# 64-slot experts: fp32 weights fed unsplit into two halves of the array's columns, and expert weights laid out in rows of 8 KB

## The chip, the cores and the metric

The kernel runs on one core of a Trainium2 chip. The metric is the device time of one execution in microseconds (us), as a median of runs; lower is better. The engines are PE (TensorE matmuls; PEld is its loading of the stationary operand), DVE (VectorE), ACT (ScalarE), POOL (GpSimd) and SP (SyncE, which here issues the DMAs).

## The reference: what is computed

Two layers on 256 frames of width 1024: a mixer (attention, short convolution and a gated recurrence) and then a channel mixer. The channel mixer of layer 0 is a dense SwiGLU, that of layer 1 has eight experts of which each frame takes two:

```python
def swiglu(x, w_gate, w_up, w_down):
    return (jax.nn.silu(x @ w_gate) * (x @ w_up)) @ w_down
...
    logits = (t @ w_router).astype(jnp.float32) + b_router.astype(jnp.float32)
    top_v, top_i = lax.top_k(logits, TOP_K)
    top_w = jax.nn.softmax(top_v, axis=-1)
    gates = jnp.sum(jax.nn.one_hot(top_i, N_EXPERTS, dtype=jnp.float32) * top_w[..., None], axis=1)
    for e in range(N_EXPERTS):
        out = out + gates[:, e:e + 1].astype(t.dtype) * swiglu(t, w_gate[e], w_up[e], w_down[e])
```

Per expert w_gate and w_up are 1024 x 3584 and w_down is 3584 x 1024, all fp32: 42 MB (of 1,048,576 bytes each) per expert, 336 MB for eight. That is most of what the kernel reads.

## The kernel before

**Stages.** From 0 to about 160 us runs mixer 0, to about 400 us the dense channel mixer, to about 540 us mixer 1, and from there to the end the experts (`moe`). All weights pass through one `Stream` (line 46): a list of halves of 1 MB (128 partitions x 2048 fp32) in the order in which they are used. `load` (L71) issues the next half on SP's queue as soon as a raw buffer is free. `high` (L99, its work at L107) rounds a half to fp32r on ACT (tile `whi`), `low` (L109, its work at L117) takes the remainder on DVE (tile `wlo`) and then frees the raw buffer. `get` (L123) is called ahead of each piece of matmuls and keeps `low` 2.5 and `high` 3.5 halves ahead of what PE uses; there are 4 `whi` and 3 `wlo` tiles. In the expert stage the raw buffers are 3 of `raw`, 4 blocks `b0` to `b3` and, for a time, `x3`, `x4` and `y`.

**Experts by rank.** `route` counts the frames of each expert and sorts them. The three fullest (`r < NBIG`) have 128 slots, the other five 64. An expert is done in 7 blocks of 512 hidden columns: 21 big and 35 small blocks. `plan_moe` (L808) puts three big blocks first and then spreads the other big ones between the small ones; the steps of neighbouring blocks interleave as gate of block i, up of block i-1, down of block i-2. The PE, ACT and DVE order of this stage is the order of the code (`manual_schedule`).

**A big block** takes the product of two split operands as three fp32r products (hi x hi, lo x hi, hi x lo). Gate and up are 24 matmuls each of 512 moving columns, down 24, so 72.

**A small block** packs the hi and lo parts of its 64 slots side by side into the 128 columns of the stationary operand (`gather`, `gather2`), so two products do: each k-tile of a weight goes through as `whi` and as `wlo`, 128x512 each. Gate 16, up 16, down 16 matmuls: 48. The two halves of 64 rows in the result have to be added: `gate` and `up_done` copy both results to SBUF (`a`, `au`), `turn` (L1002) multiplies them with a matrix of two stacked identities (`both`), which transposes and adds, and then computes silu times up on 64 columns and splits that into hi and lo again (L1018 to L1022). `down_piece` uses two banks (`ls`), and `finish` (L1036) scales them (L1043, L1044), scatters them back with 16 matmuls and adds to `xT` (L1053).

**Layout.** w_gate and w_up lie as in the reference; a half is 128 partitions x 4 k-tiles x 512 columns, so runs of 2 KB in HBM. A half of w_down is 128 partitions x 2 rows x 1024 columns, runs of 4 KB.

Of the kernel before, what the change touches and what calls it, by code (L numbers as in the profile page):

```python
# [16 lines left out]
P = 128  # L17
# [28 lines left out]
class Stream:  # L46

    def __init__(self, nc, raw, parts):  # L50
        self.nc, self.parts = nc, parts


        self.free = [(lambda: raw.tile([P, 2048], F32, name="raw"), None)] * RAW_BUFS
# [5 lines left out]
    def add(self, *halves, fine=False, wide=False):  # L60


        self.src += [(x, fine, wide) for x in halves]
        return len(self.src) // 2 - 1
# [6 lines left out]
    def load(self):  # L71
        while self.free and self.n_load < len(self.src):
            x, fine, _ = self.src[self.n_load]
# [35 lines left out]
    def low(self):  # L109
# [8 lines left out]
        if h:  # L118
            buf = self.raw.pop(i)[1]
            if buf[1] is None or self.n_load + len(self.free) < buf[1]:  # L120
                self.free.append(buf)

    def get(self, c, h):  # L123
# [6 lines left out]
        while self.n_hi < min(n + 2 * (HI_BUFS - LO_BUFS), last):  # L130
            self.high()
        n = self.hi[i].shape[1] // 2
        return self.hi[i][:, q * n:(q + 1) * n], self.lo[i][:, q * n:(q + 1) * n]


class Kern:
    def __init__(self, tc, ctx, d):
# [3 lines left out]
        self.raw = ctx.enter_context(tc.tile_pool(name="rawp", bufs=RAW_BUFS))  # L141
# [10 lines left out]
    MOE_TAGS = dict(z=2, lv=2, ls=2, S=2)  # L152
# [659 lines left out]
    def plan_moe(self, j):  # L812
# [3 lines left out]

        d = self.d
# [13 lines left out]
        def half(w, r, i, n, c):  # L831

            def view(e):
                x = w[j].rearrange("e (k p) c -> e p k c", p=P)[e, :, i:i + n, c]
                return x if r == 0 else x.rearrange("e p k c -> (e p) k c")
# [4 lines left out]
        for kind, i in steps:  # L840
            r, b = blocks[i]
            if kind != "d":
                w = d["moe_w_gate" if kind == "g" else "moe_w_up"]
                halves = (half(w, r, q, 4, slice(b * 512, (b + 1) * 512)) for q in (0, 4))
            else:
                halves = (half(d["moe_w_down"], r, 4 * b + q, 2, slice(0, D)) for q in (0, 2))
            plan[kind, r, b] = self.st.add(*halves, fine=(kind, i) == ("d", n - 1),
                                           wide=(kind, i) not in (("g", 0), ("d", n - 1)))
        return blocks, steps, plan

    def moe(self, l, plan, z):
        nc, tc = self.nc, self.tc
        blocks, steps, plan = plan
        with ExitStack() as ctx:
# [8 lines left out]
            self.st.more(lambda: spare(xbuf(4)), 2 * plan["d", 1, 3] + 2)  # L863

# [14 lines left out]
            both = big.tile([P, 64], F32, name="both")  # L879
            nc.vector.tensor_tensor(both, self.ident[:, 0:64], self.ident[:, 64:P], ALU.add)  # L880
# [17 lines left out]
            def rows(k, n, rhs):  # L898

                pg = self.bank()  # L900
                for j in range(2):
                    for t in range(2):
                        self.mm(pg[:, j * T:(j + 1) * T], (hth, htl)[n][:, t, (k + j) * P:(k + j + 1) * P], rhs(t),
                                t == 0, t == 1)
# [15 lines left out]
            def gather(ranks):  # L920

                for r, x in ranks:
                    xs[r] = xbuf(x) if r < NBIG else xbuf(x)[:, 0]

                def step(k, n):
                    pv = rows(k, n, lambda t: S[:, t].rearrange("p a b -> p (a b)"))
                    pv = pv.rearrange("p (j a b) -> p j a b", j=2, a=2)
                    for i, (r, _) in enumerate(ranks):
                        if r >= NBIG:
                            nc.scalar.activation(xs[r][:, k:k + 2, n * 64:(n + 1) * 64], pv[:, :, i, 0:64], AF.Copy)  # L930
# [9 lines left out]
            def gather2():  # L940

                pair = [xbuf(1), xbuf(2)]
                for r in range(NBIG, NE - 1):
                    xs[r] = pair[(r - NBIG) // 2][:, (r - NBIG) % 2]

                def step(k, n):
                    pv = rows(k, n, lambda t: S2[:, t, :, 0:64])
                    pv = pv.rearrange("p (j a b) -> p a j b", j=2, a=4)
                    for m in range(2):
                        nc.scalar.activation(pair[m][:, :, k:k + 2, n * 64:(n + 1) * 64], pv[:, 2 * m:2 * m + 2],  # L950
                                             AF.Copy)
# [485 lines left out]
```

## Time and profile before

| | us |
|---|---|
| median of 3 runs (lowest to highest) | 1440.64 (1440.03 to 1442.37) |
| the profiled execution's own time | 1441.26 |
| its span in the trace | 1439.5 |
| PE busy in the span | 1393.2 (97%) |
| DVE busy | 1221.7 (85%) |
| ACT busy | 1029.7 (72%) |
| bytes read | 433.20 MB, 302 GB/s over the span |

The busy shares of the page are over the whole span. The three stages ahead of the experts use the DMA queue little and the expert stage uses it without a pause, so the stages have to be read one by one. A PE that is shown busy overlaps the end of one matmul with the start of the next; how far apart matmuls start is read from the chain of work or from the timeline.

### The profile page before, as it was taken

The numbers are of one execution on the slowest core, as the hardware profiler recorded it, in microseconds if no ns is written. First come the engines' busy times: TensorE is split into PE (matmuls) and PEld (weight loads), VectorE is DVE, ScalarE is ACT, GpSimd is POOL, SyncE is SP. The second block draws the span as 40 slices with busy tenths as digits, with TensorE's granted clock in tenths as the row PEclk, the third lists the DMA queues.
The fourth block names the chain that finished last, engine by engine and source line by source line (L and its number), as shares of the span: only waits on it lengthen the run. The fifth ranks groups of instructions, "written<-read, shape, count | busy, mean of one in ns | idle before, by whom it ended". The sixth has DMA issues, their size and how long they took to land.

```text
span 1439.5 us, 21728 instructions
## 1 busy us (share of the span) xinstructions
PE 1393.2 (97%) x8323; PEld 1200.9 (83%) x8323; DVE 1221.7 (85%) x1216; ACT 1029.7 (72%) x1062; POOL 19.6 (1%) x39
## 2 busy tenths in 40 slices
PE   7999999999999997999999999999999999999997
PEld 7887999999999886787787887878888788877875
DVE  8967765555587678899989999998999999999997
ACT  8556643344474646788888788888888888888884
POOL 4000000000000000000000000000000000000000
PEclk9999999999999999999999999999999999999999
DMA  7333455555552375899999999999999999999993
GB/s 271 128 104 127 148 195 177 186 194 176 178 173 92 122 257 205 320 396 410 409 394 388 379 394 411 413 411 392 402 412 410 400 411 411 413 411 411 412 412 152
DMA packets 186766, 435.73 MB, mean 303 GB/s; under 512 B 6816, under 2 KB 11040, under 8 KB 186656
## 3 DMA queue, kind: packets, MB, share of 16 engines
q1 hardware_dynamic: 186656, 434.28, 80.0%
q8 instruction: 67, 1.10, 0.3%
q14 instruction: 43, 0.35, 0.1%
HBM read 433.20 MB, written 1.05 MB: 302 GB/s over the span
## 4 chain that ended last, share of the span: by engine, by line
PE 81%; DVE 10%; DMA 3%; ACT 2%; issue 2%; DVEq 0%; ACTq 0%
PE z L356 49%; PE S L356 12%; PE lv L356 11%; PE ls L356 7%; DVE wlo L117 5%; DMA b<-moe_w_gate 3%; ACT whi L107 1%; PE S L1007 1%; DVE y L1044 1%; DVE xT L1053 0%; DVE b L549 0%; DVE on L533 0%; PE lv L659 0%; PE S L659 0%; DVE al L1019 0%
## 5 line engine op out<-in xcount | busy, mean ns | idle before, releaser
L117 DVE TENSOR_TENSOR wlo<-raw,whi 128x1024 fp32r<-128x1024 f32 (+2 forms) x287 | 479.7, 1684 | 96.1 <-issue 50.2
L107 ACT ACTIVATE whi<-raw 128x1024 fp32r<-128x1024 f32 (+2 forms) x287 | 404.4, 1427 | 176.0 <-PE z L356 101.7
L117 DVE TENSOR_TENSOR wlo<-b,whi 128x2048 fp32r<-128x2048 f32 (+1 forms) x177 | 395.6, 2249 | 10.8 <-PE z L356 4.2
L356 PE MATMUL z<-whi,x 128*128 128x512 f32 x1232 | 366.0, 400 | 3.5 <-DVE x L936 2.6
L107 ACT ACTIVATE whi<-b 128x2048 fp32r<-128x2048 f32 (+1 forms) x177 | 332.9, 1883 | 33.9 <-PE z L356 8.9
L356 PE MATMUL z<-wlo,x 128*128 128x512 f32 x896 | 282.7, 396 | 4.6 <-DVE wlo L117 4.3
L356 PEld LDWEIGHTS z<-whi,x 128*128 128x128 f32 x1232 | 224.4, 189 | 50.3 <-DVE x L936 3.1
L356 PE MATMUL z<-hi,whi 128*128 128x256 f32 x864 | 246.5, 286 | 9.6 <-ACT whi L107 7.9
L356 PE MATMUL z<-lo,whi 128*128 128x256 f32 x864 | 246.7, 286 | 0.0
L356 PE MATMUL z<-hi,wlo 128*128 128x256 f32 x864 | 245.9, 285 | 0.0
L356 PEld LDWEIGHTS z<-wlo,x 128*128 128x128 f32 x896 | 167.3, 188 | 49.9 <-DVE wlo L117 9.9
L356 PEld LDWEIGHTS z<-hi,whi 128*128 128x128 f32 x864 | 164.1, 190 | 12.3 <-ACT whi L107 7.9
L356 PEld LDWEIGHTS z<-hi,wlo 128*128 128x128 f32 x864 | 164.0, 190 | 2.9 <-issue 2.1
L356 PEld LDWEIGHTS z<-lo,whi 128*128 128x128 f32 x864 | 164.1, 190 | 2.5 <-issue 1.3
L356 PE MATMUL ls<-whi,ah 128*128 128x512 f32 x264 | 83.8, 396 | 0.0
L356 PE MATMUL ls<-wlo,ah 128*128 128x512 f32 x264 | 83.6, 395 | 0.0
L356 PEld LDWEIGHTS ls<-wlo,ah 128*128 128x128 f32 x264 | 49.6, 188 | 12.0
L356 PEld LDWEIGHTS ls<-whi,ah 128*128 128x128 f32 x264 | 49.3, 188 | 11.6
L117 DVE TENSOR_TENSOR wlo<-x,whi 128x2048 fp32r<-128x2048 f32 x24 | 54.6, 2286 | 3.4 <-PE z L356 3.0
L356 PE MATMUL lv<-whi,ah 128*128 128x512 f32 x168 | 53.3, 395 | 0.0
L356 PE MATMUL lv<-wlo,ah 128*128 128x512 f32 x168 | 53.3, 395 | 0.0
L356 PE MATMUL lv<-whi,al 128*128 128x512 f32 x168 | 53.3, 395 | 0.0
(332 smaller groups left out, 1712.1 us busy)
## 6 DMA issues: line engine op xcount, KB each, us to landing
b<-moe_w_gate SPq DMA_DIRECT2D x59, 1024.0 KB, 9.6
b<-moe_w_up SPq DMA_DIRECT2D x57, 1024.0 KB, 10.3
b<-moe_w_down SPq DMA_DIRECT2D x56, 1024.0 KB, 10.0
raw<-moe_w_up SPq DMA_DIRECT2D x45, 1024.0 KB, 10.3
raw<-moe_w_down SPq DMA_DIRECT2D x43, 1024.0 KB, 9.6
raw<-moe_w_gate SPq DMA_DIRECT2D x42, 1024.0 KB, 9.5
raw<-w_in SPq DMA_DIRECT2D x22, 1024.0 KB, 4.9
raw<-ffn_w_gate SPq DMA_DIRECT2D x14, 1024.0 KB, 5.0
```

Of the source, the lines that this page charges most:

```text
L107: self.nc.scalar.activation(hi, x, AF.Copy)
L117: self.nc.vector.tensor_tensor(lo, x, self.hi[i][:, h * a:(h + 1) * a].bitcast(F32), ALU.subtract)
L356: self.nc.tensor.matmul(out, lhsT, rhs, start=start, stop=stop, skip_group_check=True)
L1007: nc.tensor.transpose(pt[:, q * P:(q + 1) * P], a[0][:, q * P:(q + 1) * P], self.ident)
L1044: nc.vector.scalar_tensor_tensor(y2[:, 1, c], y[c], gs[:, 0:1], y2[:, 0, c].bitcast(F32), ALU.mult, ALU.subtract)
```

## The change

It touches the expert stage and the host's layout of its weights.

1. **Layout.** The host stores each half of an expert's weight as 128 partitions x 2048 fp32 in one piece, so a partition's part is one run of 8 KB. The values are the same. In the program the DMA of a half is now 128x2048 where it was 128x4x512 or 128x2x1024. The last block's down weights still load in four parts of 0.5 MB.
2. **Small blocks take the raw fp32 weight.** `whole=True` halves are neither rounded nor split: `part` returns nothing for them, `get` returns the raw buffer, and a new `done` frees it behind PE's last matmul on it. The slots are gathered as plain fp32, 64 columns wide. For gate and up each k-tile is two matmuls with the same 64 stationary columns, one for weight columns 0 to 255 into rows 0 to 63 of the bank and one for columns 256 to 511 into rows 64 to 127: the two halves of the array's columns. For down, the two halves are the two 512-column halves of the output, in one bank.
3. **What falls away in a small block**: both splits of each weight half, the copies `a`/`au` of 512 columns, the matmuls with `both`, the hi/lo split of the activations. What comes: Silu on ACT and the product with up on DVE at once on 128x256, two transposes, one copy.
4. **Buffers.** `x2` is one more raw buffer for the whole expert stage. `ls` has one bank, `S` three.

```diff
     def part(self, n, parts, name):
         i, h = divmod(n, 2)
+        if self.src[i][3]:
+            return None, None
...
-        if h:
-            buf = self.raw.pop(i)[1]
-            if buf[1] is None or self.n_load + len(self.free) < buf[1]:
-                self.free.append(buf)
+        if h and not self.src[i][3]:
+            self.release(i)
+
+    def release(self, i):
+        buf = self.raw.pop(i)[1]
+        if buf[1] is None or self.n_load + len(self.free) < buf[1]:
+            self.free.append(buf)
...
+        if self.src[i][3]:
+            n = self.raw[i][0].shape[1] // 2
+            return self.raw[i][0][:, q * n:(q + 1) * n]
...
+    def done(self, c, h):
+        if h % 2:
+            self.release(2 * c + h // 2)
+            self.load()
...
-    MOE_TAGS = dict(z=2, lv=2, ls=2, S=2)
+    MOE_TAGS = dict(z=2, lv=2, ls=1, S=3)
...
+            self.st.more(lambda: spare(xbuf(2)))
...
+                w = self.st.get(c, h)
+                for k in ks:
+                    for i in range(2):
+                        self.mm(z[i * 64:(i + 1) * 64, 0:256], xs[r][:, k], w[:, k - 2 * h, i * 256:(i + 1) * 256],
+                                k == 0, k == KT - 1)
+                self.st.done(c, h)
...
             def gate(r, z):
+                n = 512 if r < NBIG else 256
+                a = tp.tile([P, 512], F32, name="a", bufs=2)[:, 0:n]
+                nc.scalar.activation(a, z[:, 0:n], AF.Silu, scale=sTs[r][1][:, 1:2])
+                return a
...
+                for q in range(4 if r < NBIG else 2):
+                    nc.tensor.transpose(pt[:, q * P:(q + 1) * P], a[:, q * P:(q + 1) * P], self.ident)
...
-                pv = pt.rearrange("p (m r s) -> p m r s", m=2, r=4)
-                for m in range(2):
-                    for q in range(4):
-                        self.mm(pv[:, m, q], a[m][:, q * P:(q + 1) * P], both, True, True)
-                ac = tp.tile([P, 4, 64], F32, name="al")
-                nc.scalar.activation(ac, pv[:, 0], AF.Silu)
-                nc.vector.tensor_tensor(ac, ac, pv[:, 1], ALU.mult)
...
+                x = x.bitcast(F32)[:, :, 0:64]
+                nc.scalar.activation(x.rearrange("p (i j) s -> p j i s", i=2),
+                                     pt[:, 0:256].rearrange("p (j i s) -> p j i s", j=2, i=2), AF.Copy)
+                return x
...
+                w = self.st.get(n, q)
+                for c in range(2):
+                    self.mm(y[0][c * 64:(c + 1) * 64], a[:, q], w[:, 0, c * 512:(c + 1) * 512], f, z)
+                self.st.done(n, q)
...
+    for n in ("moe_w_gate", "moe_w_up"):
+        a = g[n][0].reshape(NE, 2, 4, P, NB, 512).transpose(0, 4, 1, 3, 2, 5)
+        arrays[n] = np.ascontiguousarray(a).reshape(NE, NB, 2, P, 2048)
+    a = g["moe_w_down"][0].reshape(NE, NB, 2, 2, P, D).transpose(0, 1, 2, 4, 3, 5)
+    arrays["moe_w_down"] = np.ascontiguousarray(a).reshape(NE, NB, 2, P, 2048)
```

**PE, the down step of the first small block and the gate step of the next one.** In the rows `ls` is the down result, `z` a gate or up result, `x_6247` the gathered slots (64 of them, hi and lo, before; plain after). Before:

```order
L356 MATMUL ls<-whi,ah 128x512 x2
L356 MATMUL ls<-wlo,ah 128x512 x2
L356 MATMUL ls<-whi,ah 128x512 x2
L356 MATMUL ls<-wlo,ah 128x512 x2
L356 MATMUL z<-whi,x_6247 128x512 x2
L356 MATMUL z<-wlo,x_6247 128x512 x2
L356 MATMUL S<-both,a 128x64 x4
L356 MATMUL S<-both,au 128x64 x4
```

After:

```order
L372 MATMUL z<-raw_6618,x_6247 64x256 x8
L372 MATMUL z<-raw_6633,x_6247 64x256 x8
L372 MATMUL ls<-b_6649,ah 64x512 x4
L372 MATMUL ls<-x_6700,ah 64x512 x4
L372 MATMUL z<-x_6712,x_6247 64x256 x4
L1027 MATMUL S<-ident,a 128x128 x2
L372 MATMUL z<-x_6712,x_6247 64x256 x4
```

The split weights `whi` and `wlo` are gone from these steps, PE reads the landed buffers themselves, and eight folding matmuls have become two transposes. Stretches of 64-row results now stand between matmuls over all 128 columns: 98 such stretches in the whole expert stage.

**DVE, a stretch of one big block between small ones.** `wlo` rows are the remainders of weight halves. Before:

```order
L117 TENSOR_TENSOR wlo<-b_6784,whi 128x2048
L117 TENSOR_TENSOR wlo<-b_6802,whi 128x2048
L117 TENSOR_TENSOR wlo<-raw,whi 128x2048
L117 TENSOR_TENSOR wlo<-b_6854,whi 128x2048
L997 SCALAR_TENSOR_TENSOR a<-z,gs,a 128x512
L117 TENSOR_TENSOR wlo<-x_6872,whi 128x2048
L117 TENSOR_TENSOR wlo<-x_6891,whi 128x2048
L1011 TENSOR_TENSOR al<-S,ah 128x512
```

After:

```order
L121 TENSOR_TENSOR wlo<-b_6596,whi 128x2048
L121 TENSOR_TENSOR wlo<-b_6602,whi 128x2048
L1021 SCALAR_TENSOR_TENSOR a<-z,gs,a 128x256
L121 TENSOR_TENSOR wlo<-b_6612,whi 128x2048
L1021 SCALAR_TENSOR_TENSOR a<-z,gs,a 128x256
L121 TENSOR_TENSOR wlo<-x_6731,whi 128x2048
L121 TENSOR_TENSOR wlo<-b_6741,whi 128x2048
L1021 SCALAR_TENSOR_TENSOR a<-z,gs,a 128x512
```

Only the halves of big blocks are left to split; a small block leaves one DVE instruction of 128x256. ACT loses the matching `whi` rows.

## Rows read from the trace of the kernel before

**Rows 1.** The page: busy shares of the span, then transfers in 40 slices

```profile
PE 1393.2 (97%) x8323; PEld 1200.9 (83%) x8323; DVE 1221.7 (85%) x1216; ACT 1029.7 (72%) x1062; POOL 19.6 (1%) x39
...
GB/s 271 128 104 127 148 195 177 186 194 176 178 173 92 122 257 205 320 396 410 409 394 388 379 394 411 413 411 392 402 412 410 400 411 411 413 411 411 412 412 152
```

**Rows 2.** Three stretches of the expert stage, columns named in the first line

```profile
core 0: us, PE busy (x) PEld busy (x) DVE busy (x) ACT busy (x) POOL busy (x), PEclk, DMA share, GB/s
560.40:618.50 58.10, 56.72 (x265) 46.60 (x266) 47.40 (x36) 44.52 (x44) 0.00 (x0) 0.97 0.90 326
618.50:1417.40 798.90, 783.50 (x3763) 641.34 (x3762) 764.20 (x470) 677.09 (x529) 0.00 (x0) 1.00 1.03 403
1417.40:1439.50 22.10, 13.35 (x69) 10.41 (x67) 13.21 (x14) 7.20 (x9) 0.00 (x0) 0.91 0.15 51
```

**Rows 3.** The queue in 618.5 to 1417.4 us, then all that 1417.4:1439.5 us moved

```profile
q1 hardware_dynamic: 135158, 321.56, 103.0%
...
out<-xT SPq DMA_DIRECT2D x4, 256.0 KB, 3.5
```

**Rows 4.** Chain of work around 1008 us: start us, us, what, count

```profile
1008.67 5.60 PE lv L356 x24
...
1015.67 1.73 PE S L356 x16
...
1025.38 3.73 PE ls L356 x16
```

**Rows 5.** Splits by DVE and ACT, 640 to 1400 us: count, busy us, mean ns

```profile
L117 DVE TENSOR_TENSOR wlo<-b,whi 128x2048 fp32r<-128x2048 f32 x156 | 354.4, 2285 | 6.7 <-issue 3.3 <-PE z L356 1.4 <-ACT x L934 1.3
...
L107 ACT ACTIVATE whi<-b 128x2048 fp32r<-128x2048 f32 x157 | 300.0, 1913 | 29.9 <-PE z L356 8.0 <-PE lv L356 5.9 <-DMA b<-moe_w_gate 3.9
```

**Rows 6.** Timeline of PE at 125 us, attention's fp32 products: start us, us, what

```profile
124.98 0.28 PE L356 MATMUL S<-hi,whi 128*128 128x256 f32 x1
125.27 0.87 PE L356 MATMUL lv<-pT,b 128*64 128x256 f32 x8
126.07 0.44 PE L659 MATMUL lv<-ident,Pm 128*128 128x128 f32 x2
```

**Rows 7.** Timeline of PE at 537 us: fp32r and then fp32 matmuls of 256 columns

```profile
537.00 0.28 PE L356 MATMUL S<-hi,whi 128*128 128x256 f32 x1
537.11 0.29 PE L356 MATMUL S<-lo,whi 128*128 128x256 f32 x1
...
537.44 3.62 PE L356 MATMUL lv<-h,sm 128*8 128x256 f32 x16
540.99 0.61 PE L356 MATMUL lv<-ones,y 128*128 128x1 f32 x4
```

**Rows 8.** The queue's packets in 860:863 us, then in 1072.2:1075.2 us

```profile
DMA packets 617, 1.23 MB, mean 410 GB/s; under 512 B 16, under 2 KB 16, under 8 KB 617
...
DMA packets 325, 1.27 MB, mean 422 GB/s; under 512 B 16, under 2 KB 16, under 8 KB 325
```

**Rows 9.** What SP's queue waited for from 600 us: us, times, longest

```profile
SPq L83 <- DVE wlo L117: 545.2, 278, 4.5
```

**Rows 10.** A DMA issue line of the page: count, KB each, median us to landing

```profile
raw<-ffn_w_up SPq DMA_DIRECT2D x14, 1024.0 KB, 5.0
```

**Rows 11.** Chain of work at the end

```profile
1427.17 0.51 PE ls L356
...
1427.70 0.70 ACT y L1043
...
1428.43 0.76 DVE y L1044
...
1429.23 0.64 PE S L356 x3
```

**Rows 12.** Loads of 64 columns, 120 to 130 us: count, busy us, mean ns

```profile
L356 PEld LDWEIGHTS lv<-pT,b 128*64 128x64 f32 x16 | 1.2, 135 | 0.9 <-ACT pT L660 0.4
```

More of the change, by code (lines that the diff above doesn't have):

```diff
@@ L51, in __init__ @@
         self.nc, self.parts = nc, parts
-        self.free = [(lambda: raw.tile([P, 2048], F32, name="raw"), None)] * RAW_BUFS
+        self.free = [(lambda i=i: raw.tile([P, 2048], F32, name=f"raw{i}"), None) for i in range(RAW_BUFS)]
         self.limit = None
@@ L58, in __init__, with add @@
         self.between = []
-    def add(self, *halves, fine=False, wide=False):
-        self.src += [(x, fine, wide) for x in halves]
+    def add(self, *halves, fine=False, wide=False, whole=False):
+        self.src += [(x, fine, wide, whole) for x in halves]
         return len(self.src) // 2 - 1
@@ L841, in plan_moe @@
             r, b = blocks[i]
[L842 to L846, printed above, removed]
+            w = d["moe_w_" + dict(g="gate", u="up", d="down")[kind]]
+            halves = [half(w, r, b, q, 2 if kind == "d" else 4) for q in range(2)]
             plan[kind, r, b] = self.st.add(*halves, fine=(kind, i) == ("d", n - 1),
-                                           wide=(kind, i) not in (("g", 0), ("d", n - 1)))
+                                           wide=(kind, i) not in (("g", 0), ("d", n - 1)), whole=r >= NBIG)
         return blocks, steps, plan
@@ L878, in moe @@
             iot2 = iot[:, None, 0:64].to_broadcast([P, 2, 64])
-            both = big.tile([P, 64], F32, name="both")
-            nc.vector.tensor_tensor(both, self.ident[:, 0:64], self.ident[:, 64:P], ALU.add)
             S = big.tile([P, 2, 2, P], F32R, name="S")
@@ L896, in moe, with rows @@
             sTs, xs, acts, ys = {}, {}, {}, {}
-            def rows(k, n, rhs):
+            def rows(k, ns, rhs):
                 pg = self.bank()
+                at = [(n, t) for n in ns for t in range(2)]
                 for j in range(2):
-                    for t in range(2):
+                    for n, t in at:
                         self.mm(pg[:, j * T:(j + 1) * T], (hth, htl)[n][:, t, (k + j) * P:(k + j + 1) * P], rhs(t),
-                                t == 0, t == 1)
+                                (n, t) == at[0], (n, t) == at[-1])
                 return pg
@@ L940, in gather2, with step @@
             def gather2():
-                pair = [xbuf(1), xbuf(2)]
+                x = spare(xbuf(1)).rearrange("p (r k c) -> p r k c", r=4, k=KT)
                 for r in range(NBIG, NE - 1):
-                    xs[r] = pair[(r - NBIG) // 2][:, (r - NBIG) % 2]
-                def step(k, n):
-                    pv = rows(k, n, lambda t: S2[:, t, :, 0:64])
+                    xs[r] = x[:, r - NBIG]
+                def step(k):
+                    pv = rows(k, (0, 1), lambda t: S2[:, t, :, 0:64])
                     pv = pv.rearrange("p (j a b) -> p a j b", j=2, a=4)
-                    for m in range(2):
-                        nc.scalar.activation(pair[m][:, :, k:k + 2, n * 64:(n + 1) * 64], pv[:, 2 * m:2 * m + 2],
-                                             AF.Copy)
-                return [lambda k=k, n=n: step(k, n) for k in range(0, KT, 2) for n in range(2)]
+                    nc.scalar.activation(x[:, :, k:k + 2], pv, AF.Copy)
+                return [lambda k=k: step(k) for k in range(0, KT, 2)]
             order_of = {getattr(mybir.EngineType, n) for n in ("PE", "Activation", "DVE")}
@@ L1041, in finish @@
                 y2 = ybuf()
-                for c in range(2):
+                for c in range(len(y)):
                     nc.scalar.activation(y2[:, 0, c], y[c], AF.Copy, scale=gs[:, 0:1])
```

77 lines of the change are left out of this document (36 added, 41 removed).

## Prediction

> **What bounds the kernel now.** The page comes first: its busy shares are means over stages, and the slices say that from about 600 us on the queue moves 380 to 413 GB/s without a pause [rows 1]. So the expert stage is read alone, in three stretches [rows 2]. From 560 to 618 us PE is nearly full and the queue is not (326 GB/s): the buffers are full and the first three big blocks set the pace. From 618.5 to 1417.4 us all are full at once: PE 783.5 of 798.9 us, DVE 764.2, the queue 103% of its engines at 403 GB/s. The last 22.1 us have no weight left to land; only the output goes out [rows 3]. In such a balance nothing is won by relieving one engine. The time after is set by whichever of PE and the queue is later, so both are summed.
>
> **Differences of one run.** The sums are made against the profiled execution: span 1439.5, own time 1441.26, that is 1.8 more; the median of the runs is 0.6 below that.
>
> **PE, what goes.** Of a small block 48 matmuls of 512 columns go. In the chain of work 16 of them take 3.73 us, so 0.233 each and 11.2 per block [rows 4]. The 16 folding passes with the matrix of two identities take 1.73 us [rows 4]. Per block 12.9, for 35 blocks 452 us.
>
> **PE, what comes.** The logits tell what an unsplit fp32 matmul costs: 8 of them stand in the trace as 16 passes, started within 540.99 - 537.44 = 3.55 us [rows 7]; less about 0.1 at the end that is 0.218 per pass of 256 columns, where an fp32r matmul of 256 columns takes 0.11 to 0.12 [rows 7]. If the two halves of the array's columns ran one after the other, a k-tile would cost 4 x 0.218 = 0.87 instead of 2 x 0.233 = 0.47, and the change would lose. Attention in this same trace already does such products: `lv<-pT,b` has 64 columns of stationary operand in fp32, two heads into the two halves of one bank. Its eight passes (four of 256, four of 128 columns) begin at 125.27 and the next matmul begins at 126.07 [rows 6]: 0.80 us. One after the other they would need 4 x 0.218 + 4 x 0.109 = 1.31; side by side 0.65 plus a start and an end of 0.15. So I take side by side. Gate is then 8 k-tiles x 2 passes x 0.218 = 3.49, up the same, down 4 x 2 x 0.436 = 3.49: 10.5 per block, plus two transposes of 0.11: 10.7, for 35 blocks 374 us.
>
> **PE, the changes of width.** Ahead of the attention products a 256-column matmul starts at 124.98; by its own slot of 0.12 the next could start at 125.10, and it starts at 125.27: 0.17 lost. The 0.15 inside and some 0.08 on the first matmul behind make 0.40 per stretch of half-width matmuls [rows 6]. The order of the changed program has 98 such stretches: 39 us. Bounds: 0.17 alone (17 us), or twice my value (78 us).
>
> **PE, sum.** 452 - 374 - 39 = 39 us less. The last weight matmul ended at about 1428.1 [rows 11]; 1389 if PE waits as long as before (15.4 idle in the long stretch and 1.4 ahead of it [rows 2]), 1372 if it never waits.
>
> **DVE and ACT.** 210 of the 336 halves are no longer split: 210 x 2.285 = 480 us of DVE and 210 x 1.913 = 402 us of ACT go [rows 5]. What comes is a few instructions of 128x256 per block. Both drop far below PE and the queue; the part of PE's waits that stood behind a queue of splits on DVE should shrink.
>
> **The queue.** A half keeps its 1 MB; only its runs grow. A stretch of 3 us with 2 KB packets alone moves 410 GB/s, one with 4 KB packets alone 422 [rows 8]: per engine (16 of them) 79.9 and 155.3 ns a packet, so 75.4 for each further 2 KB and 4.5 that don't grow. By that an 8 KB packet takes 306 ns: 428 GB/s. I take 427. Bounds: 412, the flat rate of the slices now (8 KB runs bring nothing), and 433. The long stretch moved 321.56 MB [rows 3]: 753 us at 427, 780 at 412, 743 at 433. Now it takes 798.9, which is 18 over its own 412, lost where DVE or PE held back a buffer. With PE still close behind I keep 10 of those. The stretch ahead of 618.5 is big blocks on PE and stays; one more buffer lets one load out earlier, at most 2.5 us, left to the range. Last landing: 618.5 + 753 + 10 = 1381.5.
>
> **The tail.** Now 22.1 us from the last landing, as splits were still queued on ACT and DVE. Afterwards PE reads the landed part itself: two passes of 0.44 and its latency 1.1, one evacuation on ACT 0.70 and DVE 0.76 [rows 11], so 2.6, then the same scatter, adds and stores as from 1429.23 to 1439.5, 10.3. In all 12.9. Span 1381.5 + 12.9 = 1394.4; the PE side gives 1372 to 1389 and 11.4, 1383 to 1400, which agrees. Own time 1396.2, median 1395.6: **1396 us**.
>
> **The wait that is added.** SP's next load used to wait for `low` on DVE, 278 times and 545 us in all [rows 9], which hurt nobody while the queue was full. For small blocks it now waits for PE's last matmul on the half. Behind it stand only further loads. Eight buffers at 2.45 us each make a round of 19.6 us, of which a transfer with an unhurried queue takes 5.0 [rows 10]; a half may thus lie for over 14 us before the queue runs dry, and PE needs 1.75 for it.
>
> **Rivals.**
> - The halves don't run side by side in long streams as they do in eight passes. Then the 366 us of passes double, PE ends at about 1755 and the time is 1768: slower. It decides early: PE is as late as before as soon as a pair of passes takes 11% longer (39 of 366). Against it: the eight passes of two heads overlap in both halves [rows 6]. For it: those are eight passes at a time, never hundreds.
> - The loads of the stationary operand are no longer hidden. Eight loads of 0.135 each [rows 12] and eight passes fit into 0.80 us [rows 6], so they overlapped; if they had to stand between the passes, 2800 loads x 0.135 = 378 us would make it 1780. The Trainium skill (TensorE: Matmul & The Clock Gate, Part 3, "What overlaps and what doesn't") says that a load overlaps with running matmuls only where the row groups differ, and column halves share all rows. By that rule this rival would win; the trace speaks against it, with those eight loads.
> - 8 KB runs bring nothing over 412 GB/s, so this half of the change does not do what it says: 618.5 + 780 + 10 + 12.9 and the 1.2 to the median: 1423.
> - Changes of width cost twice my value, or passes run up to 10% long: PE ends at about 1428 again, 1430 to 1440.
> - Held buffers starve the queue: it needs PE to leave a half for over 14 us with the queue short of others. Then rate and time stay as they were, about 1440.
>
> **How the numbers follow.** Forecast (1380 to 1410) 0.68; no gain from 8 KB 0.12; PE late by widths or longer passes 0.07; held buffers 0.03; no overlap of halves 0.05, of loads 0.02; better than 1375 (433 GB/s and no waits) 0.03. The range 1375 to 1425 leaves out about 0.17. A run tells 0.2% (2.9 us) from no change. Faster by more than that: 0.68 + 0.12 + 0.03, most of PE late and a third of held buffers, 0.88; same 0.04; slower 0.07 of no overlap and 0.01 of held buffers, 0.08.
>
> **What would show it.** Half-width passes of `z` starting in pairs, 16 of them (gate of a block) in 3.5 us; the slices at 420 or more GB/s from about 600 to 1375 us with packets of 8 KB; DVE below 50% there; the last landing near 1381 and some 13 us behind it. It is wrong if a gate step of a small block takes 4 us or more, if the slices stay at 412, or if PE shows waits for loads while the slices dip.

## The result and the profile after

| | before | after |
|---|---|---|
| median of the runs (lowest to highest), us | 1440.77 (1440.03 to 1442.37) | 1401.12 (1400.87 to 1404.03) |
| ratio, 95% interval | | 0.973 (0.9715 to 0.9744) |
| the profiled execution's own time, its span, us | 1441.26, 1439.5 | 1400.9, 1399.2 |

The change takes 2.7% off. The forecast was 1396, the range 1375 to 1425; the time lies 5 us behind the forecast, and those 5 us are traced below.

First the page of the changed kernel: busy shares, then the transfers in 40 slices of 35 us. They answer to [rows 1].

```profile
PE 1351.3 (97%) x8953; PEld 1027.9 (73%) x8953; DVE 753.2 (54%) x967; ACT 600.3 (43%) x759; POOL 19.6 (1%) x39
...
GB/s 271 139 106 121 152 181 183 185 188 187 186 172 121 106 190 215 285 316 427 426 426 427 427 426 427 426 427 414 398 427 426 427 426 427 426 426 427 426 427 238
```

From the 19th slice on the queue moves 426 to 427 GB/s almost without a break (two slices are lower, 414 and 398), where before it moved 380 to 413. DVE and ACT have dropped to about half of the span. The same three stretches as in [rows 2], cut just behind the new last landing (1383.5 us), show who is full:

```profile
core 0: us, PE busy (x) PEld busy (x) DVE busy (x) ACT busy (x) POOL busy (x), PEclk, DMA share, GB/s
560.40:618.50 58.10, 56.30 (x283) 44.11 (x284) 34.61 (x29) 29.07 (x26) 0.00 (x0) 0.96 0.77 294
618.50:1383.80 765.30, 747.76 (x4408) 476.98 (x4406) 317.57 (x236) 269.64 (x251) 0.00 (x0) 0.99 1.00 422
1383.80:1399.20 15.40, 7.12 (x40) 3.05 (x36) 3.23 (x5) 0.69 (x1) 0.00 (x0) 0.85 0.21 73
```

The long stretch went from 798.9 to 765.3 us, the tail from 22.1 to 15.4: together the 40 us. The first stretch lost a little instead, 294 GB/s against 326. The long stretch alone, its transfers in 40 slices of 19.1 us, all its packets, and the part of the weights' queue:

```profile
GB/s 370 426 425 428 425 428 425 425 430 423 428 425 425 429 425 429 425 426 385 396 424 428 426 426 426 426 427 426 426 426 427 426 426 426 427 426 427 426 426 367
DMA packets 44546, 322.63 MB, mean 422 GB/s; under 512 B 4944, under 2 KB 4944, under 8 KB 5456
q1 hardware_dynamic: 44496, 321.93, 100.0%
```

39,090 of the packets are of 8 KB or more; they are nearly all of the bytes.

PE is still busy for 98% of the long stretch, so the page alone doesn't say which of PE and the queue now sets the pace. The PE timeline (start us, us, what, count) and the group of PE's operand loads in the same 3.6 us show how the half-width passes run, the first check that the prediction named:

```profile
1371.85 3.67 PE L372 MATMUL z<-b,x 128*64 128x256 f32 x32
1375.35 1.03 PE L372 MATMUL z<-raw,x 128*64 128x256 f32 x8
...
L372 PEld LDWEIGHTS z<-b,x 128*64 128x64 f32 x32 | 2.2, 137 | 1.1
```

The 32 passes of one step take 1375.35 - 1371.85 = 3.50 us (3.49 predicted), so 16 pairs at 0.219. Their 32 loads of 0.137 would fill 4.4 us one behind the other; they run in pairs, busy for 2.2 us in all, and fit into the same 3.50, hidden, since 16 pairs of passes at the prediction's 0.218 fill 3.49 alone.

### The profile page after: what moved, and what is told of

Same layout as the page of the kernel before. It is cut to its first block, busy times and chain, and to the rows that moved or that the text cites. A ratio compares the mean times of both kernels' runs of the same rounds, so it can differ in the third digit from the quotient of the medians.

```text
span 1399.2 us, 21895 instructions
## 1 busy us (share of the span) xinstructions
PE 1351.3 (97%) x8953; PEld 1027.9 (73%) x8953; DVE 753.2 (54%) x967; ACT 600.3 (43%) x759; POOL 19.6 (1%) x39
## 4 chain that ended last, share of the span: by engine, by line
PE 67%; DMA 18%; DVE 8%; ACT 4%; issue 1%; SPq 0%; DVEq 0%; ACTq 0%
PE z L372 41%; PE lv L372 10%; PE S L372 9%; DMA b<-moe_w_up 6%; PE ls L372 5%; DVE wlo L121 4%; DMA b<-moe_w_down 3%; ACT whi L111 3%; DMA x<-moe_w_up 2%; DMA x<-moe_w_down 2%; DMA raw<-moe_w_gate 2%; DMA b<-moe_w_gate 2%; DMA raw<-moe_w_up 1%; PE S L1027 1%; DVE b L565 0%
## 5 line engine op out<-in xcount | busy, mean ns | idle before, releaser
L121 DVE TENSOR_TENSOR wlo<-raw,whi 128x1024 fp32r<-128x1024 f32 (+2 forms) x196 | 273.8, 1417 | 120.9 <-issue 49.6
L111 ACT ACTIVATE whi<-raw 128x1024 fp32r<-128x1024 f32 (+2 forms) x196 | 231.9, 1210 | 196.0 <-PE z L372 95.0
L372 PE MATMUL z<-whi,x 128*128 128x512 f32 x672 | 192.4, 408 | 6.0 <-DVE x L954 3.9
L121 DVE TENSOR_TENSOR wlo<-b,whi 128x2048 fp32r<-128x2048 f32 (+1 forms) x63 | 139.4, 2221 | 75.1 <-ACT whi L111 70.5
L111 ACT ACTIVATE whi<-b 128x2048 fp32r<-128x2048 f32 (+1 forms) x63 | 116.6, 1857 | 90.2 <-DMA b<-moe_w_up 52.3
L372 PEld LDWEIGHTS z<-whi,x 128*128 128x128 f32 x672 | 123.4, 192 | 41.7 <-issue 6.1
L372 PE MATMUL z<-b,x 128*64 128x256 f32 x992 | 121.3, 383 | 0.0
L372 PE MATMUL z<-wlo,x 128*128 128x512 f32 x336 | 108.1, 403 | 3.3 <-DVE wlo L121 3.1
L372 PE MATMUL z<-raw,x 128*64 128x256 f32 x768 | 93.3, 382 | 0.0
L372 PEld LDWEIGHTS z<-wlo,x 128*128 128x128 f32 x336 | 63.4, 191 | 22.1 <-DVE wlo L121 7.2
```

The lines of the kernel that those rows point to most:

```text
L111: self.nc.scalar.activation(hi, x, AF.Copy)
L121: self.nc.vector.tensor_tensor(lo, x, self.hi[i][:, h * a:(h + 1) * a].bitcast(F32), ALU.subtract)
L372: self.nc.tensor.matmul(out, lhsT, rhs, start=start, stop=stop, skip_group_check=True)
```

## The experiments

The theory after the result: the queue alone sets the pace from about 620 us to the last landing, PE follows with some per cent to spare, and what is missing to the forecast went at the two ends. Its rivals: PE is the bound (the 98% are real), or only one half of the change matters. Each version ran beside the kernel before, whose median lay between 1440.25 and 1441.35 us; the changed kernel was not run again beside them. Where a version's interval of the ratio overlaps the changed kernel's (0.9715 to 0.9744), the difference between the two isn't clear of the noise.

### Each half of the change alone

`e1_layout_only` is the kernel before with the 8 KB layout and nothing else.

```diff
-        def half(w, r, i, n, c):
+        def half(w, r, b, q, n):
...
+    for n in ("moe_w_gate", "moe_w_up"):
+        a = g[n][0].reshape(NE, 2, 4, P, NB, 512).transpose(0, 4, 1, 3, 2, 5)
+        arrays[n] = np.ascontiguousarray(a).reshape(NE, NB, 2, P, 2048)
...
```

> The kernel before with nothing but the 8 KB layout: all splits, folding passes and buffers as before. Theory (PE and DVE bind as closely as the queue, so relieving the queue alone wins little): PE was idle 15.4 us in the long stretch, so at most that is won, 1427 to 1438 us, the queue's rate in the long stretch stays near 403 to 408 GB/s although each packet is faster. Rival A (the queue alone was the bound): the whole step from 410 to 427 GB/s shows, 1410 to 1416. Rival B (the layout slows something): 1441 or more.

Measured: 1437.43 (1435.2 to 1437.99) against 1441.35 of the kernel before in the same comparison, ratio 0.9973 (0.9963 to 0.9982). The layout alone is worth 3.9 us, as the theory said. Its slices, and its long stretch in the columns of [rows 2]:

```profile
GB/s 265 135 104 120 162 189 178 191 189 177 179 173 91 122 257 188 320 397 419 420 361 396 383 392 426 426 413 355 410 427 426 374 413 425 426 426 393 426 426 134
...
618.50:1417.40 798.90, 787.14 (x3790) 645.57 (x3789) 767.49 (x472) 678.65 (x531) 0.00 (x0) 1.00 0.99 404
```

The queue can move 426 now and does so in single slices, but it is held again and again (361, 355, 374): the mean is 404, before it was 403. DVE (767.5 of 798.9) and PE (787.1) have no time for more.

`e2_unsplit_only` is the changed kernel with the layout of before.

```diff
-                return w[e, b, q].rearrange(("" if r == 0 else "e ") + "p (k c) -> " +
-                                            ("p" if r == 0 else "(e p)") + " k c", k=n)
+                x = w[j].rearrange("e (k p) c -> e p k c", p=P)[e, :, i:i + n, c]
+                return x if r == 0 else x.rearrange("e p k c -> (e p) k c")
...
```

> The changed kernel with the weights laid out as before (runs of 2 and 4 KB); PE, ACT, DVE and buffers as changed. Theory (after the change the queue alone sets the pace): the long stretch takes its bytes at 411 to 414 GB/s, about 780 us, with PE waiting for weights more often: 1419 to 1427 us. Rival A (PE is the bound after the change, 8 KB rows bring nothing): within 3 us of 1401. Rival B (unsplit weights win nothing without the layout): 1436 to 1441.

Measured: 1430.98 (1428.15 to 1435.46), ratio 0.9936 (0.9911 to 0.9961). Its slices:

```profile
GB/s 258 144 104 119 151 203 178 178 184 193 184 177 89 95 261 230 273 368 410 413 411 411 412 411 411 413 397 348 399 412 412 411 412 412 411 413 412 411 411 256
```

The flat rate is the 411 to 413 that was expected, so the queue is the bound; the time is 4 us above the theory's range. The slice of 348 (965 to 1000 us) is where to look. Stretches of 4 us ahead of it and in it (columns as above), then ACT's and PE's timelines there, with the idle time ahead of an instruction and what ended it in brackets:

```profile
938.00:942.00 4.00, 1.51 (x14) 0.72 (x10) 0.00 (x0) 1.54 (x1) 0.00 (x0) 1.00 1.05 416
942.00:946.00 4.00, 2.79 (x10) 1.77 (x12) 3.02 (x3) 3.13 (x4) 0.00 (x0) 0.62 1.02 416
946.00:950.00 4.00, 4.00 (x13) 2.75 (x10) 3.32 (x3) 0.47 (x1) 0.00 (x0) 0.50 1.05 408
950.00:954.00 4.00, 4.00 (x11) 2.75 (x10) 0.69 (x1) 2.85 (x2) 0.00 (x0) 0.50 1.05 410
954.00:958.00 4.00, 4.00 (x11) 2.75 (x10) 2.10 (x2) 0.97 (x1) 0.00 (x0) 0.50 1.04 416
958.00:962.00 4.00, 4.00 (x14) 2.29 (x14) 1.99 (x3) 0.00 (x0) 0.00 (x0) 0.75 0.99 398
962.00:966.00 4.00, 4.00 (x21) 1.98 (x18) 1.75 (x1) 0.00 (x0) 0.00 (x0) 1.00 0.84 277
...
994.00:998.00 4.00, 4.00 (x22) 1.52 (x22) 0.95 (x2) 0.38 (x1) 0.00 (x0) 1.00 0.19 26
```

```profile
940.46 1.91 ACT L111 ACTIVATE whi<-b 128x2048 fp32r<-128x2048 f32 x1 [10.38 <-DMA b<-moe_w_up]
942.27 0.67 ACT L1069 ACTIVATE y<-ls,gs 128x512 fp32r<-128x512 f32 x1
...
935.79 0.60 PE L372 MATMUL ls<-b,ah 128*64 128x512 f32 x2
...
943.00 0.58 PE L372 MATMUL S<-sT,y 64*128 64x256 f32 x1 [3.49 <-ACT y L1069]
```

PE runs out of work because ACT stood 10.38 us in front of a weight half that had not landed, and the small instruction that PE needed (`y`) was queued behind it, though its input `ls` was complete at 936.4. PE idles 3.49 us, and from 943 to some 960 us its granted clock is 0.50, the lower of its two levels (1.2 instead of 2.4 GHz). It then takes twice as long over each half, the halves stay in their buffers, and at 962 us the queue itself runs dry (277 GB/s), after SP had waited 10.1 us for one of PE's down matmuls. So a queue that starves PE is later held up by PE.

That is the smaller part of the slice. The larger is at 994 to 998 us, 26 GB/s, with PE at its full clock, and the changed kernel dips at the same place of its order, also at full clock. SP's waits for `ls` from 920 to 1020 us (us, times, longest), here and then in the changed kernel, and its dip:

```profile
SPq L84 <- PE ls L372: 20.1, 4, 10.1
```

```profile
SPq L84 <- PE ls L372: 27.0, 8, 8.6
...
978.00:982.00 4.00, 4.00 (x26) 1.64 (x24) 0.37 (x1) 0.00 (x0) 0.00 (x0) 1.00 0.76 262
```

There a big block's gate step, with the gather of the next expert's slots between its matmuls, stands between two small steps, and SP waits (8.6 us in the changed kernel) until PE has done it. Against its flat rate the queue loses some 7.7 us here between 962 and 1006 us, and 3.3 in the changed kernel between 974 and 990. How much of the difference is due to the lower clock was not separated.

Over the long stretch the mean clock of this kernel is 0.97, and the 322.6 MB that 783 us would do for at 412 GB/s take 796.5:

```profile
618.50:1415.00 796.50, 764.48 (x4409) 487.03 (x4407) 317.79 (x236) 269.81 (x251) 0.00 (x0) 0.97 1.03 405
```

The two halves of the change are worth 3.9 and 10.4 us alone, 14.3 in all, and 40 together.

### Where the passes' price lies

`e3_one_half` puts both halves of a gate or up weight into the same 64 columns of the array. It leaves out a part of these sums (which part, and how it is lost, was not traced); the matmuls are all there.

```diff
-                        self.mm(z[i * 64:(i + 1) * 64, 0:256], xs[r][:, k], w[:, k - 2 * h, i * 256:(i + 1) * 256],
+                        self.mm(z[0:64, i * 256:(i + 1) * 256], xs[r][:, k], w[:, k - 2 * h, i * 256:(i + 1) * 256],
...
```

> The changed kernel with the gate and up passes of a small block all in the first 64 columns of the array: columns 0 to 255 and 256 to 511 of a weight into two halves of one row range of the bank, one after the other; evacuation on 64 partitions, four transposes instead of two; down unchanged. Theory (the two halves of the columns run side by side in long streams): gate and up each cost twice 3.49 us instead of once, 7.0 us per block, 244 for 35 blocks, less the 17 us that PE idles now: 1615 to 1645 us, PE the bound, the queue's rate near 320 GB/s. Rival (the halves already run one after the other, or the passes' price is not in the columns): 1400 to 1410.

Measured: 1617.6 us (one run), within the theory's range. Its PE timeline:

```profile
909.66 3.67 PE L372 MATMUL z<-raw,x 128*64 128x256 f32 x16
913.16 3.40 PE L372 MATMUL z<-x,x 128*64 128x256 f32 x15
```

Here 16 passes take 3.50 us, where the changed kernel does 32 in the same time. Side by side in gate and up is thus worth 217 us of 1401, and without it the change would lose.

### How late PE is by itself

`e4_half_bytes` loads only the first half of each weight half of the 64-slot experts and lets PE read that twice: it leaves out half of these weights.

```diff
-            for j in range(0, a, n):
+            for j in range(0, a // 2 if self.src[self.n_load][3] else a, n if not self.src[self.n_load][3] else a // 2):
...
-            return self.raw[i][0][:, q * n:(q + 1) * n]
+            return self.raw[i][0][:, 0:n]
```

> The changed kernel with only the first half of each weight half of the 64-slot experts loaded, and read twice by PE: it leaves out half of these experts' weights; PE, ACT and DVE do as much as in the changed kernel. It shows how late PE would be if the queue were no bound. Theory (the queue binds by about 2%, PE stands close behind): span 1370 to 1388 us, PE idle under 5 us in the long stretch. Rival A (PE had much slack, waits hid in its busy time): under 1360. Rival B (PE was the bound already): 1396 or more.

Measured: 1370.2 us (one run), span 1368.4. The stretch from 618.5 us to the end of its last weight matmul, and that matmul's line of the timeline:

```profile
618.50:1357.50 739.00, 739.00 (x4428) 473.95 (x4424) 315.17 (x236) 264.68 (x251) 0.00 (x0) 1.00 0.81 294
...
1356.07 1.89 PE L373 MATMUL ls<-b,x 128*64 128x512 f32 x8
```

With the queue out of the way PE never idles in this stretch and never leaves its full clock, and the kernel is 31 us faster. So PE was not the bound: it could have ended some 31 us earlier. The span sits just below the theory's 1370 to 1388, because PE's work is shorter than the prediction's sum (last weight matmul ended at 1358.0 instead of 1372).

`e9_more_pe` asks the same the other way round and gives PE more to do.

```diff
-                    nc.tensor.transpose(pt[:, q * P:(q + 1) * P], a[:, q * P:(q + 1) * P], self.ident)
+                    for _ in range(1 if r < NBIG else 3):
+                        nc.tensor.transpose(pt[:, q * P:(q + 1) * P], a[:, q * P:(q + 1) * P], self.ident)
```

> The changed kernel with each of the two transposes of a small block done three times over, the same result written again: four more passes of 0.11 to 0.14 us per block, 15 to 20 us more work on PE in all, and nothing more for any other engine or the queue. Theory (the queue sets the pace and PE idles 17.5 us of the long stretch, spread over it): most of it goes into that idle time, 1401 to 1409 us, and PE, waiting less, falls to half its clock less often. Rival A (PE and the queue bind together, each us of PE is a us of time): 1416 to 1421. Rival B (PE kept busy keeps its clock, which pays for the work): below 1401.

Measured: 1403.68 (1401.82 to 1404.85), ratio 0.9744 (0.9727 to 0.9762), 2.6 us above the changed kernel for 140 more passes at 0.11, some 15 us of PE. The intervals overlap, so that the cost is small is shown, and its size is not. Its long stretch and what follows, to be held against those of the changed kernel above:

```profile
618.50:1383.80 765.30, 752.75 (x4536) 487.59 (x4534) 317.17 (x236) 269.73 (x251) 0.00 (x0) 1.00 1.01 421
1383.80:1399.20 15.40, 9.24 (x50) 3.75 (x46) 3.23 (x5) 0.69 (x1) 0.00 (x0) 0.86 0.23 78
```

PE's busy time rises by 5.0 us in the long stretch and by 2.1 behind it, for more work than that: the mean clock is 1.00 where it was 0.99, since of the five short stretches at half clock in the changed kernel one is left. Two of those five, in the changed kernel:

```profile
889.40:892.80 3.40, 3.40 (x9) 2.65 (x8) 1.83 (x1) 0.13 (x1) 0.00 (x0) 0.50 1.01 426
...
1357.00:1360.40 3.40, 3.40 (x9) 2.64 (x9) 2.11 (x2) 0.00 (x0) 0.00 (x0) 0.50 1.01 426
```

### The length of a row

`e5_rows_4k` gives all expert weights rows of 4 KB.

```diff
...
-        arrays[n] = np.ascontiguousarray(a).reshape(NE, NB, 2, P, 2048)
...
+        a = np.ascontiguousarray(a).reshape(NE, NB, 2, P, 2, 1024).transpose(0, 1, 2, 4, 3, 5)
+        arrays[n] = np.ascontiguousarray(a)
...
```

> The changed kernel with every expert weight in rows of 4 KB instead of 8 KB, nothing else. Theory (after the change the queue alone sets the pace, by its packets): 422 GB/s instead of 427 makes the long stretch 9 us longer, and PE, waiting a little more often, may run at half its clock more often, which costs up to 5 more: 1409 to 1416 us. Rival A (any long row will do, 4 KB is as good): within 3 us of 1401. Rival B (it is 8 KB or nothing): 1425 to 1431, as with the rows of before.

Measured: 1413.02 (1411.58 to 1417.19), ratio 0.9811 (0.9792 to 0.983), in the middle of the theory's range. Its slices:

```profile
GB/s 275 132 106 120 151 196 191 181 179 179 183 178 119 90 226 234 274 333 419 421 420 420 420 419 421 420 420 384 410 420 420 420 420 419 421 420 414 420 420 237
```

Rows of 2 and 4 KB, of 4, and of 8 give 412, 420 and 427 GB/s and 1431, 1413 and 1401 us. The time follows the queue's rate over all three, as it must where the queue sets the pace.

### Changes of width, the start and the tail

`e6_turn_at_change` moves a small block's transposes, where it can, to the edge of a step that is 128 columns wide.

```diff
+                    big = [r < NBIG or n < NBIG for n in (blocks[max(i - 3, 0)][0], blocks[i - 1][0])]
+                    at = 0 if r < NBIG else 3 if big[1] else -1 if big[0] else 0
-                    for h in range(4):
-                        piece(up_piece, z, kind, r, b, h)
-                        if kind == "g" and h == 0 and i > 1:
+                    for h in range(-1, 4):
+                        if h >= 0:
+                            piece(up_piece, z, kind, r, b, h)
+                        if kind == "g" and h == at and i > 1:
```

> The changed kernel with the transposes of a small block's activations moved, where a neighbouring step is 128 columns wide, to the edge of that step: 79 stretches of half-width matmuls instead of 98, the work the same. At 0.3 to 0.4 us a stretch PE is 6 to 8 us shorter. Theory (PE has 2% to spare, the queue sets the pace, only the tail and the waits for buffers feel it): 1396 to 1400 us. Rival A (PE and the queue hold each other up, so PE's whole saving counts): 1393 to 1395. Rival B (the widths cost nothing that matters): within 1 us of 1401.

Measured: 1404.07 (1398.68 to 1410.06), ratio 0.9747 (0.9721 to 0.9774). All three expectations missed: no gain, and the runs spread over 11 us, across the changed kernel's. With less work PE ran dry for longer: in the profiled execution (1401.2) it idled 22.0 us of the long stretch instead of 17.5. The five runs' times and mean clocks are 1398.7 at 0.987, 1401.2 at 0.984, 1404.1 at 0.984, 1405.6 at 0.986 and 1410.1 at 0.977: the slowest has the lowest clock and the fastest the highest, though the three between don't line up.

`e7_two_lead` puts two big blocks ahead of the small ones instead of three, one step at a time, so that the same twelve halves load before the ranks are known.

```diff
-LEAD = 3
+LEAD = 2
...
+        steps = [(k, i) for k in "gud" for i in range(2)] + [
+            (k, i - j) for i in range(2, n + 2) for j, k in enumerate("gud") if 2 <= i - j < n]
...
```

> The changed kernel with two big blocks ahead of the small ones instead of three, done one step at a time (both gates, both ups, both downs) so that the same twelve halves are loaded before the experts' ranks are known; the other 19 big blocks are spread as before. The queue ran at 294 GB/s while PE worked on the three big blocks (560 to 618 us); that stretch gets one block, 16.8 us, shorter, 5 us of queue time. Theory (the big blocks at the start hold the buffers and cost the queue its time): the slices reach 420 GB/s some 16 us earlier, 1394 to 1398 us. Rival A (the start is bound by when the ranks are known, or the one-after-the-other steps leave gaps on PE): 1400 to 1406. Rival B (PE is bound anyway): 1401.

Measured: 1396.29 (1396.12 to 1397.66), ratio 0.9693 (0.9678 to 0.9707): the theory. What it mends is seen in SP's timeline and waits of the changed kernel, 560 to 640 us:

```profile
606.05 1.93 SPq L84 DMA_DIRECT2D raw<-moe_w_up  x2
609.94 0.33 SPq L84 DMA_DIRECT2D b<-moe_w_down  x1
618.59 0.33 SPq L84 DMA_DIRECT2D x<-moe_w_down  x1
...
SPq L84 <- PE z L372: 23.3, 5, 8.1
```

From 609.94 to 618.59 no load goes out: SP waits for PE's last matmul on a small half (8.1 us the longest), and PE is busy with the big blocks. The stretch 600 to 620 us, in the changed kernel and then in this one:

```profile
600.00:620.00 20.00, 20.00 (x124) 14.39 (x122) 8.99 (x8) 7.38 (x8) 0.00 (x0) 1.00 0.70 285
```

```profile
600.00:620.00 20.00, 20.00 (x152) 13.33 (x150) 6.05 (x6) 9.23 (x9) 0.00 (x0) 1.00 0.92 373
...
1381.89 1.89 PE L372 MATMUL ls<-raw,x 128*64 128x512 f32 x8
```

The last landing comes at 1380.0 instead of 1383.5, and PE's last weight matmul, the second row, ends 3.8 us behind it instead of 5.1: the tail is shorter too.

`e8_both` is the last two edits together.

> The last two edits together (two big blocks ahead, transposes at the edges of wide steps; 89 half-width stretches). Theory (the queue starts 5 us earlier and PE is shorter, so both add): 1389 to 1395 us. Rival A (only one of the two bounds gives way): 1396 to 1399. Rival B (neither matters): 1400 to 1402.

Measured: 1396.15 (1394.81 to 1398.2), ratio 0.9688 (0.9675 to 0.9702): rival A. It is the start's gain alone; fewer changes of width bring nothing.

`e10_no_x2` takes the additional raw buffer away.

```diff
-            self.st.more(lambda: spare(xbuf(2)))
```

> The changed kernel without its additional raw buffer (x2 unused): one buffer fewer for the whole expert stage. Theory (small halves are held until PE has read them; with eight buffers the queue ran dry only for moments, so with seven it does so more often): the stretch to 618 us loads one half less, 2.5 us, and the long stretch falls from 422 to between 415 and 420 GB/s: 1405 to 1415 us. Rival A (buffers are plenty): within 2 us of 1401. Rival B (held buffers are the bound): over 1420.

Measured: 1408.15 (1403.13 to 1413.22), ratio 0.9789 (0.9761 to 0.9816). The median lies in the theory's range; the profiled execution is its fastest, 1403.1. It shows the lost load of the theory: to 618.5 us it has moved 110.9 MB where the changed kernel has moved 112.0, one half less, and at 421 GB/s in the long stretch it doesn't make that good. The half lands behind 1383.8 us (146 GB/s there against 73), and the last landing is at 1387.9:

```profile
1383.80:1399.20 15.40, 9.35 (x50) 3.86 (x46) 3.23 (x5) 0.69 (x1) 0.00 (x0) 0.86 0.39 146
```

The rate of the long stretch, 415 to 420 in the theory, did not fall here. That the buffer is worth about 7 us is measured; where the slower runs lose more than this one wasn't seen.

`e11_tail` ends the stage with six small blocks in a row instead of three.

```diff
-            at = [min(k * len(more) // (len(less) - 3), len(more)) for k in (i, i + 1)]
+            at = [min(k * len(more) // (len(less) - 6), len(more)) for k in (i, i + 1)]
```

> The changed kernel with the big blocks spread over 29 of the small ones instead of 32, so that six small blocks without a big one between them end the stage instead of three; nothing else (109 half-width stretches instead of 98). In the changed kernel PE worked without a gap from 1356 us to 5 us behind the last landing, because the last big block's down step came so late. Theory (that backlog is what makes the end 15.4 instead of 12.9 us): a small block takes PE 12 us and the queue 14.7, so three more of them let PE catch up, the last matmul ends 1 to 2.5 us behind the last landing, 1397 to 1399 us. Rival A (the tail's length has another cause): the last matmul stays 4 to 5 us behind, 1400 to 1402. Rival B (denser big blocks ahead of it hold buffers and cost the queue more than the tail gives): 1402 to 1406.

Measured: 1396.86 (1396.48 to 1399.05), ratio 0.97 (0.9686 to 0.9715): the theory. PE's timeline at the end, first of the changed kernel, then of this one:

```profile
1354.71 0.62 PE L372 MATMUL lv<-whi,al 128*128 128x512 f32 x2
1356.47 0.82 PE L372 MATMUL lv<-wlo,ah 128*128 128x512 f32 x2 [1.14 <-DVE wlo L121]
...
1362.55 0.40 PE L372 MATMUL lv<-wlo,ah 128*128 128x512 f32 x1
1362.88 1.08 PE L372 MATMUL z<-raw,x 128*64 128x256 f32 x8
1363.90 0.44 PE L1027 MATMUL S<-ident,a 128*128 128x128 f32 x2
1364.26 1.08 PE L372 MATMUL z<-raw,x 128*64 128x256 f32 x8
...
1386.70 1.89 PE L372 MATMUL ls<-b,x 128*64 128x512 f32 x8
```

```profile
1378.80 1.94 PE L372 MATMUL ls<-x,x 128*64 128x512 f32 x8 [0.44 <-DMA x<-moe_w_down]
...
1383.75 1.08 PE L372 MATMUL ls<-raw,x 128*64 128x512 f32 x4 [0.17 <-DMA raw<-moe_w_down]
```

In the changed kernel the last big block's down step waits for its split at 1356 us, runs partly at half clock, and PE then works without a gap to 1388.6, 5 us behind the last landing (1383.5). With three more small blocks behind it PE has caught up: it waits for the landings themselves, the last of which is at 1383.4 as before, and ends 1.4 us behind it. The span is 3.9 us shorter.

`e12_two_lead_tail` has the edits of the start and of the tail.

> The same edit on the version with two big blocks ahead. Theory: start and tail are separate, so both gains add, 1391.5 to 1395 us. Rival A (the start's gain had already shortened the tail, since PE was less behind there): 1395.5 to 1397. Rival B (denser big blocks cost the queue more than that): 1398 or more.

Measured: 1394.02 (1392.99 to 1395.71), ratio 0.9681 (0.9668 to 0.9694). The time is in the theory's range, but the gains add in part only: 4.8 and 4.3 alone, 7.1 together, as rival A has it in kind, since the version with two big blocks ahead had the tail shorter by 1.3 us already. It is the fastest version, 0.5% below the changed kernel, and its slices stay at 418 to 428 from 626 us to the last one.

## Why the prediction was right, and where it was off

**What bounds the kernel** was right: PE, DVE and the queue full at once, so that one relieved alone wins little. The single halves show it: 3.9 and 10.4 us, against 40. The prediction had priced the second of them, 8 KB rows without an effect, at 1423; it is 1431. Of the 8 us, some 3 are bytes still to move at 618.5 us, 3.5 the rate lost in the long stretch beyond the 10 us allowed (796.5 against 783), where PE's lower clock behind its waits and the buffers that it holds come in, and 1 the tail.

**PE's passes** were right to the hundredth (3.50 us for 32 passes, 3.49 predicted), on the evidence of eight passes of attention [rows 6]. The last digit is luck: (3.55 - 0.1) / 16 is 0.216 a pass, not 0.218. The rival with the loads between the passes, at 1780, is out: 32 loads of 0.137 run inside 3.50 us. The Trainium skill (TensorE: Matmul & The Clock Gate, Part 3, "What overlaps and what doesn't") says that a load overlaps with running matmuls only where the row groups differ. The trace differs from that here, with those 32 loads.

**PE's sum** was too cautious: 39 us less were predicted, so a last weight matmul at 1372 if PE never waits; the kernel with half of the bytes shows 1358.0. Of the 14 us some 10 are the changes of width. At 1362.55 a full-width pass of 0.233 is followed by a half-width one after 0.33, at 1362.88 eight passes worth 0.87 take 1.02, and two transposes worth 0.22 take 0.36 with the way back into half width: about 0.10 into, 0.15 out of and 0.05 behind, 0.3 for a stretch where 0.40 was taken. The other 4 us are open. It changed nothing, as PE wasn't the bound.

**DVE and ACT**: 480 and 402 us less were predicted, 468 and 429 were measured. But that PE's waits would shrink with them was wrong: PE idles 17.5 us in the long stretch, before 15.4 [rows 2]. It no longer waits behind a full DVE but, through ACT's and DVE's splits, for halves that haven't landed. The longest of its waits and of ACT's in the long stretch (us, times, longest):

```profile
PE lv L372 <- DVE wlo L121: 5.5, 6, 1.1
...
ACT whi L111 <- DMA b<-moe_w_up: 52.3, 14, 8.8
```

**The queue**: 427 GB/s predicted from packets of 2 and 4 KB [rows 8], 427 measured. The 10 us of held buffers came out in size: 322.63 MB at 427 are 755.6 us, and the stretch took 765.3. That is in part luck, since they went elsewhere than was meant: by the slices above 2.6 us in the first one (370 GB/s), still the start, 2.7 in the last (367), where the queue runs out, and only 3.3 in the two of 385 and 396, where buffers are held in the run of blocks. What failed is the step that let the first stretch stay as it is: it moved 294 instead of 326 GB/s, 1.9 MB or 4.4 us of queue time, because the first small halves now wait for PE while PE still has big blocks to do. The wait was seen and priced (a half may lie for 14 us), but for a stage where small blocks follow each other, not for the place where they stand behind three big ones. Most of it was made good ahead of 560 us (169 GB/s up to there, before 167), but the last landing came at 1383.5 instead of 1381.5: the weights' queue had 0.37 MB more to move in the long stretch than was forecast, 0.9 us, and the sum had left out the 0.7 MB of the other queues, 1.6 us; the allowance for held buffers was half a microsecond too large. The version with two big blocks ahead gets 4.8 us back.

**The tail**: 12.9 us predicted from the last landing, 15.7 measured (1383.5 to 1399.2). The failing term is the 1.1 us from the last landing to the end of PE's last matmul; it was 5.1, since PE still had the last big block's work before it. With that block three small ones earlier it is 1.4. A second term erred the other way: scatter, adds and stores took 9.0 us (from 1390.2 on) where 10.3 had been taken.

These two, some 2 us and 2.8, are the 4.8 by which the span (1399.2) lies above its forecast (1394.4). The median is 0.2 above the profiled run here, where it was 0.6 below it before.

**Rivals**: halves one after the other is what `e3_one_half` builds for gate and up, and it is slower by the whole of it. Held buffers exist in small (the start, the dip near 980 us, and one buffer worth 7 us), not as the bound. PE as the bound falls with `e4_half_bytes` and `e9_more_pe`. Of the chances, those outside 1375 to 1425 add up to 0.20, where 0.17 was said. Whether PE's shorter work or the freed DVE let the queue run was not separated.

## What to carry to other kernels

Where several engines are full at once, sum each of them anew for the changed program and expect the parts of a change to be worth little alone and much together. When the sum says that a queue will set the pace, look next at the two ends: what holds its buffers while it starts, and what the consumer still has to do when the last byte lands; here both were a matter of where the heavy blocks stand, and worth 7 us. Less work for a consumer with a few per cent to spare gained nothing here: 1404.1 with it and 1401.1 without, 1396.2 and 1396.3 in the version with two big blocks ahead.

## What the runs showed of the hardware that was not expected

- PE, starved for a moment, can lose more than that moment. After waits of 0.4 to 1.9 us its granted clock was 0.50 (1.2 GHz) for 3.4 us at five places of the changed kernel; after other such waits (1.1 us at 1073) it stayed at 1.00. In the kernel with the old layout it was 0.50 for 17 us from 943 us on, and the queue then ran at 277 GB/s for want of buffers. 15 us of additional work on PE cost 2.6 us, not clear of the noise, while some 6 us less of it, an estimate from 19 stretches fewer at 0.3, gained nothing.
- Two fp32 streams into the two halves of the array's columns run at the price of one over whole steps (32 passes of 256 columns in 3.50 us), with the loads of both hidden.
- Each change between half-width and full-width matmuls cost PE about 0.10 to 0.15 us beyond the passes, in the steps from 1362.55 to 1364.26 us.
- In the kernel with the old layout ACT stood 10.4 us in front of a split whose half had not landed, and the small instruction behind it (`y`), whose input was complete at 936.4 us, began at 942.3, behind the split; PE waited for it.
